# Top-k search of a sparse attention layer: counts, candidates, norm powers and the place of the selections

## The chip, the cores and the metric

The kernel runs on one core of a Trainium2 chip. The metric is the device time of one execution in microseconds (us). TensorE (PE in the profile) multiplies matrices, VectorE (DVE), ScalarE (ACT) and GpSimd (POOL, here "Pool") work element by element, SyncE (SP) issues the transfers. Each engine works through its own queue in order, and waits on semaphores for the others.

## What is computed

Two transformer layers over 1024 tokens of width 1024, in float32. The change lies in the first layer, which has two attentions side by side: A, where an indexer scores every key for each query and only the 256 best keys of the query are attended to, and B, a sliding window. The second layer is not touched.

```python
def layer_ab(x, norm_g, w_in, a_qk_norm, a_kidx_norm, b_qk_norm, b_sinks, w_out):
    y = rms_norm(x, norm_g) @ w_in
    qa, ka, va, qi, ki, wi, za, qb, kb, vb, zb = split_cols(y, AB_SPLITS)
    ...
    qi = apply_rope(qi.reshape(bsz, seq, IDX_HEADS, IDX_DIM), icos, isin)
    ki = apply_rope(rms_norm(ki, a_kidx_norm)[:, :, None, :], icos, isin)[:, :, 0]
    k_sel = min(DSA_TOPK, seq // 4)
    oa = dsa_attention(qa, ka, heads(va, A_KV_HEADS), qi, ki, wi, k_sel)
    ...
    ob = swa_sink_attention(qb, kb, heads(vb, B_KV_HEADS), b_sinks)
    mix = jnp.concatenate([oa * jax.nn.silu(za), ob * jax.nn.silu(zb)], axis=-1)
    return x + mix @ w_out

# in dsa_attention, for each block of 128 queries
        logits = jnp.einsum('bqhd,bsd->bqhs', qib, ki).astype(jnp.float32)
        score = jnp.einsum('bqh,bqhs->bqs', wib, jax.nn.relu(logits)) * idx_scale
        causal = key_pos[None, :] <= t[:, None]
        score = jnp.where(causal[None], score, -jnp.inf)
        _, idx = lax.top_k(score, k_sel)
        ...
        p = masked_softmax(s, valid[:, :, None, None, :])
```

## The kernel before

Tokens are tiled in eight blocks of 128. Projections are done as three products of split operands (`whi`, `wlo` are the two parts of a weight, from L446 on ScalarE and L447 on Pool). The first layer runs in this order: five calls of `norm_x` normalize the input (two per pair of blocks later); the columns `ki` and `qi` are projected; `scores()` computes the index scores of query blocks 2 to 7 (blocks 0 and 1 have no more than 256 keys) and cuts each into two 16-bit halves, `hi` and `lo` (L802 to L819); then the top-k search runs as an auxiliary generator, `tk = topk()`, beside the remaining projections and beside attention B; then attention A.

`Lanes` holds these strands together. `run(main, fill, ratio, aux, arate)` takes steps of a main strand, of a filling strand (projections) and of an auxiliary strand (`tk`) by the costs that each step yields; `post` hands over a short strand, and `tick` advances every posted strand by one step. The order in which the steps are written is the priority; the order on each engine is then fixed by the scheduler of the framework at build time, so it isn't a table that is written by hand.

The search finds, for each query, the 256th largest score by bits: 16 rounds over the `hi` halves, one more count, a masking of the `lo` halves (L877), 16 rounds over `lo`. Each round sets `cand` from the threshold `K` (L850), counts the scores at or above it in six blocks, compares the six counts with their targets (`inc`, L856) and moves `K` (L857). A count of block i reads (i + 1) x 128 columns. `GDA` gives its first list of blocks to VectorE (L845, a comparison with a sum) and its second to ScalarE (L841, a sign with a sum). Before, VectorE counts blocks 2, 3, 4 and 7 (384, 512, 640 and 1024 columns), ScalarE 5 and 6 (768 and 896).

When `K` is found, each block's selection makes its mask: seven VectorE instructions (L889 to L895) and two on Pool (L896, L897), which write the mask over the block's `hi`. Attention A's blocks 2 to 7 wait for their masks, its score reduce is L639 (`nm`) and its scores are L636. In the kernel before, `now(tk)` takes the rest of the search and all six selections to the end before attention A is written.

`rstd` (L270 to L289) turns sums of squares into reciprocal square roots: a start value from the bits of the number and two correction steps, nine small VectorE instructions (L277, L278, L280, L281, L283, L284, L286, L287, L288). In the first layer it is called 33 times: five times by the first norms, 28 times by head chains, the strands that norm and rotate the heads of a projection and end in operands for TensorE (`qs`, `ka`, `kb`; `ss` is their sum of squares, `nz` the normed head). `E` and `ENG` say which of some element-wise steps go to Pool; `ENG2` replaces it for the second layer.

## Time and profile before

| what | us |
|---|---|
| median of three runs (lowest, highest) | 1560.41 (1559.73, 1562.62) |
| the profiled execution | 1559.19 |
| its span | 1557.4 |
| first and last comparison of the search (L856) start at | 179.6 and 413.3 |

The difference between the profiled execution and its span is what lies around the first and last instruction. A row of a table by stretch gives, for one part of the span, the time that each engine was busy; a row of a group of instructions gives its count, busy time and mean, and the idle time of the engine just before them with what ended it. Counts of instructions stand after an x. L numbers are lines of the kernel before.

### The profile page before, as it was taken

The numbers are of one execution on the slowest core, as the hardware profiler recorded it, in microseconds if no ns is written. First come the engines' busy times: TensorE is split into PE (matmuls) and PEld (weight loads), VectorE is DVE, ScalarE is ACT, GpSimd is POOL, SyncE is SP. The second block draws the span as 40 slices with busy tenths as digits, with TensorE's granted clock in tenths as the row PEclk, the third lists the DMA queues.
The fourth block names the chain that finished last, engine by engine and source line by source line (L and its number), as shares of the span: only waits on it lengthen the run. The fifth ranks groups of instructions, "written<-read, shape, count | busy, mean of one in ns | idle before, by whom it ended". The sixth has DMA issues, their size and how long they took to land.

```text
span 1557.4 us, 35155 instructions
## 1 busy us (share of the span) xinstructions
PE 1384.3 (89%) x12588; PEld 1273.9 (82%) x12588; DVE 1226.1 (79%) x3827; ACT 869.8 (56%) x2385; POOL 821.4 (53%) x1097
## 2 busy tenths in 40 slices
PE   6998888788637889999999999999999778889999
PEld 6888878788636779999999998899988556778887
DVE  8599999999998876428338668976689999996763
ACT  6354576577406766325424666956667666754531
POOL 4767642467777657324447343565456565652240
PEclk9999999989867999999999999999999879989999
DMA  6311212111102132332312210012100210111232
GB/s 199 86 35 32 57 56 71 43 36 33 45 17 69 59 107 76 111 108 86 82 36 55 66 49 8 9 47 63 33 15 19 78 62 15 32 55 59 95 112 75
DMA packets 88431, 93.19 MB, mean 60 GB/s; under 512 B 20928, under 2 KB 73152, under 8 KB 88256
## 3 DMA queue, kind: packets, MB, share of 16 engines
q1 hardware_dynamic: 88256, 90.95, 19.3%
q8 instruction: 99, 1.62, 0.4%
q14 instruction: 76, 0.62, 0.1%
HBM read 67.85 MB, written 23.07 MB: 58 GB/s over the span
## 4 chain that ended last, share of the span: by engine, by line
PE 48%; DVE 33%; DMA 6%; POOL 5%; issue 5%; ACT 3%; SPq 0%; POOLq 0%; DVEq 0%; ACTq 0%
PE psS L636 8%; PE pp L490 7%; PE pp L492 6%; PE pp L491 6%; PE psT L664 6%; DVE junk L845 6%; DVE pt L639 4%; PE pp L1683 2%; PE pp L1681 2%; PE pp L1682 2%; PE po L684 2%; PE po L682 2%; PE po L683 2%; DMA wraw<-in_ab_w_in 1%; POOL wlo L447 1%
## 5 line engine op out<-in xcount | busy, mean ns | idle before, releaser
L490 PE MATMUL pp<-whi,Rh 128*128 128x256 f32 (+4 forms) x1648 | 489.1, 297 | 25.9 <-DVE zst L581 9.9
L492 PE MATMUL pp<-whi,Rl 128*128 128x256 f32 (+4 forms) x1648 | 481.0, 292 | 0.6 <-DVE Rl L327 0.6
L491 PE MATMUL pp<-wlo,Rh 128*128 128x256 f32 (+4 forms) x1648 | 480.0, 292 | 0.0
L490 PEld LDWEIGHTS pp<-whi,Rh 128*128 128x128 f32 x1648 | 322.5, 196 | 33.1 <-DVE zst L581 13.9
L644 ACT ACTIVATE pt<-pt,nm 128x256 f32<-128x256 f32 (+8 forms) x384 | 246.6, 643 | 178.6 <-DVE nm L639 173.3
L492 PEld LDWEIGHTS pp<-whi,Rl 128*128 128x128 f32 x1648 | 321.1, 195 | 2.2 <-DVE Rl L327 1.1
L491 PEld LDWEIGHTS pp<-wlo,Rh 128*128 128x128 f32 x1648 | 322.0, 196 | 1.0
L447 POOL TENSOR_TENSOR wlo<-wraw,whi 128x256 fp32r<-128x256 f32 (+4 forms) x208 | 162.3, 787 | 189.6 <-ACT whi L446 176.9
L664 PE MATMUL psT<-identf,pt 128*128 128x128 f32 x1256 | 216.1, 284 | 14.2 <-DVE pl L669 4.2
L674 POOL TENSOR_SCALAR ph<-sg 128x512 f16<-128x512 f32 (+3 forms) x157 | 89.3, 570 | 157.9 <-ACT sg L673 142.0
L664 PEld LDWEIGHTS psT<-identf,pt 128*128 128x128 f32 x1256 | 147.3, 143 | 28.1 <-issue 4.3
L675 POOL TENSOR_TENSOR pl<-sg,ph 128x512 f16<-128x512 f32 (+3 forms) x157 | 163.4, 1041 | 8.7
L446 ACT ACTIVATE whi<-wraw 128x256 fp32r<-128x256 f32 (+4 forms) x208 | 83.7, 416 | 125.0 <-DMA wraw<-in_cd_w_in 37.8
L669 DVE SCALAR_TENSOR_TENSOR pl<-psT,ph 128x512 f16<-128x512 f32 (+3 forms) x233 | 128.4, 556 | 26.8 <-ACT ph L668 26.4
L668 ACT ACTIVATE ph<-psT 128x512 f16<-128x512 f32 (+3 forms) x233 | 111.9, 492 | 51.7 <-PE psT L664 49.2
L684 PEld LDWEIGHTS <-pl 128*128 128x128 f16 x1256 | 114.2, 99 | 26.1 <-issue 7.4
L682 PEld LDWEIGHTS <-ph 128*128 128x128 f16 x1256 | 116.7, 100 | 20.0 <-issue 7.9
L683 PEld LDWEIGHTS <-ph 128*128 128x128 f16 x1256 | 116.7, 100 | 14.7 <-issue 13.5
L639 DVE CUSTOM_DVE_ANT_0 pt<-psS,mk 128x512 f32<-128x512 f32 (+4 forms) x208 | 107.1, 518 | 23.7 <-PE psS L636 21.8
L673 ACT ACTIVATE sg<-psT 128x512 f32<-128x512 f32 (+3 forms) x157 | 83.4, 534 | 32.7 <-PE psT L664 30.1
L344 POOL TENSOR_TENSOR nz<-nz,rs_y 128x512 f32<-128x512 f32 (+2 forms) x44 | 41.2, 937 | 94.0 <-DVE rs_y L288 68.2
L636 PE MATMUL psS<-ka,qs 128*128 128x512 f32 (+4 forms) x192 | 58.7, 405 | 24.1 <-DVE nm L639 23.8
(311 smaller groups left out, 3622.4 us busy)
## 6 DMA issues: line engine op xcount, KB each, us to landing
wraw<-in_cd_w_in SPq DMA_DIRECT2D x72, 128.0 KB, 2.1
wraw<-in_ab_w_in SPq DMA_DIRECT2D x56, 128.0 KB, 2.2
xs<-in_x SPq DMA_DIRECT2D x8, 512.0 KB, 6.0
od<-mx SPq DMA_DIRECT2D x32, 128.0 KB, 1.8
wraw<-in_ab_w_out SPq DMA_DIRECT2D x32, 128.0 KB, 2.2
x<-in_x SPq DMA_DIRECT2D x8, 512.0 KB, 4.6
mo<-od SPq DMA_DIRECT2D x16, 256.0 KB, 2.7
nz<-zdr SPq DMA_DIRECT2D x16, 256.0 KB, 2.8
```

What stands on the lines that cost most here:

```text
L447: G.tensor_tensor(lo[:, :o], raw[:, :o], hi[:, :o].bitcast(F32), OP.subtract)
L490: T.matmul(ps, xh, hi[:, :n], start=q == 0 and k == 0, stop=False)
L491: T.matmul(ps, xh, lo[:, :n], start=False, stop=False)
L492: T.matmul(ps, xl, hi[:, :n], start=False, stop=q == 3 and k == 1)
L636: T.matmul(ps[:, at + a - c:at + b - c], lhs, rhs(a, b), start=n == 0, stop=n == len(pl_) - 1)
L639: V.tensor_tensor_reduce(pt[:, j * nk + c:j * nk + c + w], ps[:, at:at + w], mask(c, w), -1.0, first, op0=OP.add, op1=OP.min, accum_out=low)
L644: S.activation(pt[:, j * nk:(j + 1) * nk], pt[:, j * nk:(j + 1) * nk], AF.Exp, scale=-1.0, bias=nm[:, h:h + 1], accum_out=sm[:, h:h + 1])
L664: T.transpose(pT[:, a], pt[:, o:o + P], identf)
L675: G.tensor_tensor(pl[:, :n], sg[:, :n], ph[:, :n], OP.subtract)
L682: T.matmul(dst, ph[:, a], vh(kt, h), start=kt == 0, stop=False)
L683: T.matmul(dst, ph[:, a], vl(kt, h), start=False, stop=False)
L684: T.matmul(dst, pl[:, a], vh(kt, h), start=False, stop=kt == nt - 1)
```

## The change

There are four parts. (1) `GDA` gives blocks 3 and 4 to ScalarE too, so VectorE counts blocks 2 and 7 and ScalarE blocks 3, 4, 5 and 6. (2) The search carries the candidate itself in place of the threshold: Pool computes `less`, the candidate minus half a step, while the counts run; then `inc` and one VectorE instruction, `cand = inc * step + less`, end the round, in place of `inc`, `K` and `cand`. The comparisons are turned round (less than, and the sign of a negated input), and `K` is made once at the end of each search. (3) In the first layer `rstd` becomes two Pool instructions, a scaling and a power with exponent -0.5 from a constant tile. (4) In place of `now(tk)` the search alone is taken to its end, and the strand with the six selections is posted, so that its steps are written between the steps of attention A.

```diff
--- before.py
+++ after.py
@@ -53,7 +53,7 @@
-GDA = [2, 3, 4, 7], [5, 6]
+GDA = [2, 7], [3, 4, 5, 6]
@@ -70,7 +70,7 @@
-ENG = 'nz zc ky'
+ENG = 'nz zc ky rs'
...
+    half = cst.tile([P, 16], F32, name="half")
+    G.memset(half, -0.5)
@@ -274,6 +276,12 @@
         t = st.tile([P, 16], F32, name="rs_t")[:, :n]
         w = ss.shape[0]
         v, y, t = v[:w], y[:w], t[:w]
+        if E["rs"] is G:
+            G.tensor_scalar(v, ss, inv * RG * RG, EPS * RG * RG, op0=OP.mult, op1=OP.add)
+            G.tensor_tensor(y, v, half[:w, :n], OP.pow)
+            yield
+            res.append(y)
+            return
         V.tensor_scalar(v, ss, inv, EPS, op0=OP.mult, op1=OP.add)
         V.tensor_scalar(y.bitcast(I32), v.bitcast(I32), -0.5, float(0x5F3759DF), op0=OP.mult, op1=OP.add)
         yield
@@ -821,6 +829,8 @@
     GD, GA = GDA
+    searched = []
     def topk():
@@ -833,52 +843,53 @@
         cnt = tkp.tile([P, 6], F32, name="cnt")
         tgt = tkp.tile([P, 6], F32, name="tgt")
         inc = tkp.tile([P, 6], F32, name="inc")
-        sgn = tkp.tile([P, 6], F32, name="sgn")
+        less = tkp.tile([P, 6], F32, name="less")
         def counts(src):
             for i in GA:
                 n = (i + 1) * P
-                S.activation(junka[:, :n], blk(src, i), AF.Sign, bias=cand[:, i - 2:i - 1],
+                S.activation(junka[:, :n], blk(src, i), AF.Sign, scale=-1.0, bias=cand[:, i - 2:i - 1],
                              accum_out=cnt[:, i - 2:i - 1])
             for i in GD:
                 n = (i + 1) * P
-                V.tensor_scalar(junk[:, :n], blk(src, i), cand[:, i - 2:i - 1], None, op0=OP.is_ge, op1=OP.add,
+                V.tensor_scalar(junk[:, :n], blk(src, i), cand[:, i - 2:i - 1], None, op0=OP.is_lt, op1=OP.add,
                                 accum_out=cnt[:, i - 2:i - 1])
-        def setcand(K, b):
-            V.scalar_tensor_tensor(cand, K, float(b), sgn, op0=OP.add, op1=OP.mult)
         def search(K, src):
             for b in range(15, -1, -1):
-                setcand(K, 1 << b)
+                if b:
+                    G.tensor_scalar(less, cand, 1.0, -float(1 << (b - 1)), op0=OP.mult, op1=OP.add)
                 counts(src)
-                V.tensor_tensor(inc, cnt, tgt, OP.is_ge)
-                V.scalar_tensor_tensor(K, inc, float(1 << b), K, op0=OP.mult, op1=OP.add)
+                V.tensor_tensor(inc, cnt, tgt, OP.is_le)
+                if b:
+                    V.scalar_tensor_tensor(cand, inc, float(1 << b), less, op0=OP.mult, op1=OP.add)
+                else:
+                    V.tensor_tensor(cand, inc, cand, OP.add)
                 yield 2000
-        V.memset(K1, -32768.5)
-        V.memset(K0, -0.5)
-        V.memset(tgt, float(TOPK))
-        V.memset(sgn, 1.0)
-        for i in GA:
-            V.memset(tgt[:, i - 2:i - 1], float(2 * TOPK - (i + 1) * P))
-            V.memset(sgn[:, i - 2:i - 1], -1.0)
+            V.tensor_scalar(K, cand, -0.5, None, op0=OP.add)
+        V.memset(cand, -0.5)
+        for i in range(2, NT):
+            n = (i + 1) * P
+            V.memset(tgt[:, i - 2:i - 1], float(n - TOPK if i in GD else n - 2 * TOPK))
         yield from search(K1, hi16)
-        setcand(K1, 1)
         counts(hi16)
         for i in range(2, NT):
             V.tensor_scalar(tgt[:, i - 2:i - 1], cnt[:, i - 2:i - 1], -1.0,
-                            float(TOPK if i in GD else 2 * TOPK - 2 * (i + 1) * P), op0=OP.mult, op1=OP.add)
-        V.tensor_scalar(K1, K1, 0.5, None, op0=OP.add)
+                            2.0 * (i + 1) * P - (TOPK if i in GD else 2 * TOPK), op0=OP.mult, op1=OP.add)
+        V.memset(cand, 32767.5)
         yield 2000
         for i in range(2, NT):
             V.scalar_tensor_tensor(blk(lo16, i), blk(hi16, i), K1[:, i - 2:i - 1], blk(lo16, i),
                                    op0=OP.is_equal, op1=OP.mult)
             yield 800
         yield from search(K0, lo16)
-        V.tensor_scalar(K0, K0, 0.5, None, op0=OP.add)
+        searched.append(1)
         for i in range(2, NT):
             n = (i + 1) * P
@@ -1111,7 +1122,10 @@
     FM = fa_then()
     L.run(attn_gen(jobs(job_b, 0, BO[0]) + jobs(job_b, 1, BO[1])), FA, BR, aux=tk, arate=TA)
-    now(tk)
+    while not searched:
+        next(tk)
+        L.tick()
+    L.post(tk)
     L.run(attn_gen(jobs(job_a, 0, AO[0]) + jobs(job_a, 1, AO[1])), FM, AR)
     L.pump(FM)
     L.flush()
```

The scheduler's order changes with it. VectorE, two rounds late in the search over `lo` before; `rs_v`, `rs_y` and `rs_t` are the norm chain, `ka` a head chain's operand:

```order
L845 TENSOR_SCALAR junk,cnt<-lo_837,cand 128x384
L286 SCALAR_TENSOR_TENSOR rs_t<-rs_y 128x8
L399 TENSOR_TENSOR ka_4544<-psT,ka_4544 128x256
L845 TENSOR_SCALAR junk,cnt<-lo_838,cand 128x512
L287 TENSOR_TENSOR rs_t<-rs_t,rs_v 128x8
L845 TENSOR_SCALAR junk,cnt<-lo_838,cand 128x640
L288 SCALAR_TENSOR_TENSOR rs_y<-rs_t,rs_y 128x8
L338 TENSOR_REDUCE ss<-sq 128x8
L845 TENSOR_SCALAR junk,cnt<-lo_838,cand 128x1024
L277 TENSOR_SCALAR rs_v<-ss 128x8
L856 TENSOR_TENSOR inc<-cnt,tgt 128x6
L278 TENSOR_SCALAR rs_y<-rs_v 128x8
```

VectorE in two late rounds of the changed kernel:

```order
L855 TENSOR_SCALAR junk,cnt<-lo_790,cand 128x384
L855 TENSOR_SCALAR junk,cnt<-lo_791,cand 128x1024
L377 TENSOR_TENSOR qs<-psT,qs 64x512 x2
L346 TENSOR_REDUCE ss<-sq 128x8
L364 TENSOR_TENSOR nz<-nz,rp_t 128x512
L866 TENSOR_TENSOR inc<-cnt,tgt 128x6
L868 SCALAR_TENSOR_TENSOR cand<-inc,less 128x6
L855 TENSOR_SCALAR junk,cnt<-lo_790,cand 128x384
L855 TENSOR_SCALAR junk,cnt<-lo_791,cand 128x1024
L866 TENSOR_TENSOR inc<-cnt,tgt 128x6
L868 SCALAR_TENSOR_TENSOR cand<-inc,less 128x6
L855 TENSOR_SCALAR junk,cnt<-lo_790,cand 128x384
```

The norm chain and two of the four counts are gone, and `nz`, `qs` and `ss` of later head chains stand between the counts.

ScalarE, two rounds late in the search before (`whi` is a weight split, `sg` a copy of scores of attention B, `nz` and `sq` start a head chain):

```order
L841 ACTIVATE junka,cnt<-lo_838,cand 128x768
L422 ACTIVATE nz<-pp 128x256
L424 ACTIVATE sq<-pp 128x256
L841 ACTIVATE junka,cnt<-lo_838,cand 128x896
L673 ACTIVATE sg<-psT 128x512
L841 ACTIVATE junka,cnt<-lo_838,cand 128x768
L422 ACTIVATE nz<-pp 128x256
L424 ACTIVATE sq<-pp 128x256
L446 ACTIVATE whi<-wraw 128x256
L841 ACTIVATE junka,cnt<-lo_838,cand 128x896
L398 ACTIVATE ka_4543<-psT 128x256
L446 ACTIVATE whi<-wraw 128x256
```

ScalarE at the same place in the changed kernel:

```order
L851 ACTIVATE junka,cnt<-lo_791,cand 128x512
L851 ACTIVATE junka,cnt<-lo_791,cand 128x640
L851 ACTIVATE junka,cnt<-lo_791,cand 128x768
L851 ACTIVATE junka,cnt<-lo_791,cand 128x896
L851 ACTIVATE junka,cnt<-lo_791,cand 128x512
L851 ACTIVATE junka,cnt<-lo_791,cand 128x640
L851 ACTIVATE junka,cnt<-lo_791,cand 128x768
L851 ACTIVATE junka,cnt<-lo_791,cand 128x896
L851 ACTIVATE junka,cnt<-lo_791,cand 128x512
L851 ACTIVATE junka,cnt<-lo_791,cand 128x640
L851 ACTIVATE junka,cnt<-lo_791,cand 128x768
L851 ACTIVATE junka,cnt<-lo_791,cand 128x896
```

The counts of several rounds now follow one another with nothing between, and copies that stood between the counts before stand ahead of them.

VectorE in the selection of the second block before:

```order
L889 TENSOR_SCALAR junk<-hi_836,K_1536 128x512
L890 SCALAR_TENSOR_TENSOR sel,cnt<-lo_838,K_1537,junk 128x512
L369 TENSOR_TENSOR qs<-psT,qs 64x512 x2
L891 TENSOR_SCALAR inc<-cnt 128x1
L892 TENSOR_SCALAR junk<-lo_838,K_1537 128x512
L338 TENSOR_REDUCE ss<-sq 128x8
L893 SCALAR_TENSOR_TENSOR sel<-hi_836,K_1536,junk 128x512
L277 TENSOR_SCALAR rs_v<-ss 128x8
L894 SCALAR_TENSOR_TENSOR junk<-sel 128x512
L278 TENSOR_SCALAR rs_y<-rs_v 128x8
L895 SCALAR_TENSOR_TENSOR sel<-junk,inc,sel 128x512
L280 TENSOR_TENSOR rs_t<-rs_y 128x8
```

VectorE in the selections of the changed kernel:

```order
L900 TENSOR_SCALAR junk<-hi_789,K_1454 128x512
L901 SCALAR_TENSOR_TENSOR sel,cnt<-lo_791,K_1455,junk 128x512
L902 TENSOR_SCALAR inc<-cnt 128x1
L903 TENSOR_SCALAR junk<-lo_791,K_1455 128x512
L904 SCALAR_TENSOR_TENSOR sel<-hi_789,K_1454,junk 128x512
L905 SCALAR_TENSOR_TENSOR junk<-sel 128x512
L906 SCALAR_TENSOR_TENSOR sel<-junk,inc,sel 128x512
L900 TENSOR_SCALAR junk<-hi_789,K_1454 128x640
L901 SCALAR_TENSOR_TENSOR sel,cnt<-lo_791,K_1455,junk 128x640
L902 TENSOR_SCALAR inc<-cnt 128x1
L903 TENSOR_SCALAR junk<-lo_791,K_1455 128x640
L904 SCALAR_TENSOR_TENSOR sel<-hi_789,K_1454,junk 128x640
```

The selections follow one another without the norm chains and `qs` that stood between; the score reduces of attention A (`pt,nm`) come in the sixth selection in both orders.

## Rows read from the trace of the kernel before

**Rows 1.** Page of the profile, part 1: busy time, share of the span, instructions.

```profile
PE 1384.3 (89%) x12588; PEld 1273.9 (82%) x12588; DVE 1226.1 (79%) x3827; ACT 869.8 (56%) x2385; POOL 821.4 (53%) x1097
```

**Rows 2.** Table by stretch: stretch, its length, busy times and counts, TensorE clock, DMA.

```profile
0.00:92.00 92.00, 74.69 (x540) 72.02 (x541) 63.76 (x183) 46.11 (x120) 56.07 (x105) 0.96 0.44 132
92.00:180.00 88.00, 74.97 (x535) 70.34 (x534) 85.03 (x180) 38.91 (x108) 59.36 (x70) 0.96 0.13 34
180.00:413.50 233.50, 194.40 (x1653) 185.97 (x1652) 229.11 (x726) 155.80 (x431) 124.26 (x162) 0.93 0.17 49
413.50:475.00 61.50, 25.51 (x162) 23.14 (x160) 61.10 (x101) 10.03 (x29) 47.08 (x42) 0.65 0.11 35
475.00:560.00 85.00, 75.10 (x818) 61.63 (x817) 72.96 (x216) 64.57 (x159) 52.44 (x67) 0.91 0.21 64
```

**Rows 3.** Timeline of VectorE, 0 to 20 us: start, duration, instruction, idle time before.

```profile
5.71 0.15 DVE L277 TENSOR_SCALAR rs_v<-ss 128x1 f32<-128x1 f32 x1 [4.41 <-ACT pt L510]
...
9.89 1.76 DVE L516 SCALAR_TENSOR_TENSOR pt<-xs,rs_y,gx 128x1024 f32<-128x1024 f32 x1
```

**Rows 4.** Busy time by stretch of L277 alone, then of L288 alone.

```profile
92.00:180.00 88.00, 3.10 (x7) 0.96 0.13 34
180.00:413.50 233.50, 4.69 (x12) 0.93 0.17 49
...
92.00:180.00 88.00, 2.01 (x8) 0.96 0.13 34
180.00:413.50 233.50, 1.74 (x11) 0.93 0.17 49
```

**Rows 5.** Groups of VectorE, 180 to 413.5 us: busy, mean, then idle time before.

```profile
L845 DVE TENSOR_SCALAR_CACHE_REDUCE junk<-lo,cand 128x640 bf16<-128x640 uint16 x16 | 13.9, 872 | 0.1
...
L845 DVE TENSOR_SCALAR_CACHE_REDUCE junk<-lo,cand 128x512 bf16<-128x512 uint16 x16 | 11.8, 735 | 0.0
...
L850 DVE SCALAR_TENSOR_TENSOR cand<-K,sgn 128x6 f32<-128x6 f32 x32 | 10.1, 315 | 0.4
```

**Rows 6.** Groups of ScalarE, 180 to 413.5 us.

```profile
L644 ACT ACTIVATE pt<-pt,nm 128x256 f32<-128x256 f32 x53 | 26.8, 506 | 20.5 <-DVE nm L639 20.4
...
L841 ACT ACTIVATE junka<-lo,cand 128x896 int8<-128x896 uint16 x16 | 16.7, 1041 | 0.1
...
L841 ACT ACTIVATE junka<-lo,cand 128x768 int8<-128x768 uint16 x16 | 15.0, 935 | 16.3 <-DVE cand L850 6.9 <-DVE rs_t L280 3.5 <-DVE rs_y L284 1.6
...
L841 ACT ACTIVATION_READ_ACCUMULATOR junka<-lo,cand 128x1 f32 x32 | 6.2, 193 | 0.0
```

**Rows 7.** Groups of VectorE, 413.5 to 475 us.

```profile
L894 DVE TENSOR_TENSOR_SCAN junk<-sel 128x384 f16<-128x384 bf16 (+5 forms) x6 | 10.2, 1706 | 0.0
...
L369 DVE TENSOR_TENSOR qs<-psT,qs 64x512 fp32r<-64x512 f32 x4 | 2.8, 690 | 0.1
L356 DVE TENSOR_TENSOR nz<-nz,rp_t 128x512 f32<-128x512 f32 x4 | 2.7, 676 | 0.0
L281 DVE TENSOR_TENSOR rs_t<-rs_t,rs_v 128x8 f32<-128x8 f32 x3 | 2.0, 683 | 0.0
...
L891 DVE TENSOR_SCALAR inc<-cnt 128x1 f32<-128x1 f32 x6 | 0.9, 146 | 0.0
...
L287 DVE TENSOR_TENSOR rs_t<-rs_t,rs_v 128x8 f32<-128x8 f32 x3 | 0.4, 148 | 0.0
```

**Rows 8.** Waits from 413.5 to 600 us: total, times, longest.

```profile
PE psS L636 <- DVE nm L639: 23.8, 10, 15.9
```

**Rows 9.** Groups of Pool: two sizes of product, the second from 92 to 180 us.

```profile
L320 POOL TENSOR_TENSOR rp_t<-ydup,cs 128x16 f32<-128x16 f32 x8 | 1.9, 235 | 10.4 <-DVE ydup L1379 10.1
...
L322 POOL TENSOR_TENSOR nz<-nz,cs 128x512 f32<-128x512 f32 x4 | 5.7, 1424 | 0.2
```

**Rows 10.** Summary of line L856: duration min/median/max in ns, first and last start.

```profile
L856 DVE TENSOR_TENSOR inc<-cnt,tgt x32: 133/162/1073, 179.6 to 413.3; 128x6 f32<-128x6 f32 x32
```

**Rows 11.** Waits from 180 to 413.5 us: total, times, longest.

```profile
ACT junka L841 <- DVE cand L850: 20.1, 14, 3.6
```

More of the change, by code (lines that the diff above doesn't have):

```diff
@@ L166, in trunk @@
     L = Lanes()
-    E = {n: G if n in ENG.split() else V for n in "nz zc qy ky dk dq dr dy".split()}
+    E = {n: G if n in ENG.split() else V for n in "nz zc qy ky dk dq dr dy rs".split()}
     cst = ctx.enter_context(tc.tile_pool(name="cst", bufs=1))
```

## The prediction

> **What bounds the kernel now.** I read the totals first, then a table of busy times by stretch, then the groups of instructions inside the stretches that the change touches, then the waits. Over the whole span TensorE is the busiest engine [rows 1], and a reader could stop there. The table by stretch says otherwise [rows 2]: from 92 to 180 us (index scores) VectorE is busy 85.0 of 88 us and TensorE 75.0; from 180 to 413.5 us (the search) VectorE 229.1 of 233.5, TensorE 194.4, ScalarE 155.8, Pool 124.3; from 413.5 to 475 us (the selections) VectorE 61.1 of 61.5 and TensorE 25.5 at a clock of 0.65. So these 383 us are VectorE's. Behind 600 us, up to 1200, TensorE is nearly full, and the change touches nothing there; it can only move the start of that part. The question is how much VectorE time leaves these three stretches, and who is next.
>
> The profiled run took 1559.19 us (span 1557.4), the median of the three runs is 1560.41: I make the sum on the profiled run and add 1.2 us at the end.
>
> **First norms, 0 to 92 us.** Nine small VectorE instructions per call become two on Pool. The first chain starts at 5.71 us and the product that uses it at 9.89 [rows 3], 4.2 us with TensorE still waiting for its first operand. Two Pool instructions of about 0.25 us (price below) with their handovers are about 1 us. The first call gains some 3 us; the four that follow overlap with weight loads, and in the Pool order the third and later pairs stand behind weight splits, which takes part of it back. I take **-2** (bounds -5 to +2).
>
> **Index scores, 92 to 180 us.** The nine lines of the norm chain hold VectorE 23.3 us here; first and last of them are in [rows 4] (3.10 and 2.01 us). They go. VectorE then needs 62 of 88 us, TensorE 75.0 and Pool 59.4 plus 16 new instructions, 4 to 8 us. TensorE is next, so at most 88 - 75 = 13 us can go. I take **-10** (bounds -13 to -3: the first score blocks also wait for chains that only got shorter).
>
> **The search, 180 to 413.5 us.** Per round VectorE loses the 512 and the 640 column counts: 0.74 + 0.87 us and one accumulator read each, about 1.65 us, over the 31 rounds here 51 us [rows 5]. It loses one of three small instructions per round, 10.1 us of `cand` lines [rows 5], and the norm chains, 26.6 us (4.69 us in the first of the nine lines, 1.74 in the last [rows 4]). 229 - 51 - 10 - 27 = 141; the order shows some 10 to 20 us of head work (`nz`, `qs`, `ss`) drawn in from the selections, so 150 to 165.
>
> ScalarE gains the two counts. Its counts of 768 and 896 columns take 0.935 and 1.041 us [rows 6], 0.1 us for 128 columns; carried down, 640 and 512 columns take 0.83 and 0.72, each with an accumulator read of 0.19 of which half overlaps: about 1.75 us a round, 54 us. 155.8 + 54 = 210, and the order draws in ten or so copies that stood behind the last count before: about 222 us. **ScalarE is next**, and it is nearly as full as VectorE was. A sum of the rows of each round in the new order gives the same: the larger of the two engines, round by round, adds up to 224 us.
>
> It can't fill every gap. Each round ends with a handover (last count, `inc`, `cand`, first count): an accumulator read of 0.19 us [rows 6], two small instructions of 0.16 [rows 10] and the steps between engines, by my estimate 0.9 us in all. The last rounds have nothing on ScalarE between the counts: 3.9 us of counts and 0.9, about 4.8 us each. Some ten such rounds add 9 us, and the counts stand in order behind exponentials that wait for VectorE (20.5 us of idle time before the group L644 [rows 6]). I take 238 us, **+4**, with bounds 222 (all gaps filled) and 260 (222, and the idle time that the groups of [rows 6] show before them, some 37 us, all stays). So the counts moved to ScalarE hardly pay by themselves: they exchange one full engine for another.
>
> `less` on Pool adds a wait: it needs `cand`, and behind it on Pool stand weight splits, `ph`/`pl` and the norm pairs. It is due only a whole round later and Pool is 53% busy, so I cost it at nothing; if Pool comes late by 1 us in each of 30 rounds, it is 30 us, half of it hidden by ScalarE's own waits.
>
> **The selections, 413.5 to 475 us.** Seven lines, 10.2 us for the longest and 0.9 for the shortest [rows 7], add up to 44.8 us. The other 16 us of VectorE here are norm chains (10.6, nine lines between 2.0 and 0.4), `qs` (2.8), `nz` (2.7) and small things [rows 7]; the norm chains go, the rest now stands ahead of the last counts. The order shows the first five selections in one unbroken block behind `K`, and only the sixth among the first scores of attention A, just as before. So posting them doesn't put them beside attention; the stretch shrinks to its own work: 61.5 to about 44.5, **-17** (bounds -12 to -22, the longer one if the port is quieter).
>
> **Attention A's start, 475 to 560 us.** VectorE 73 of 85 us, TensorE 75 [rows 2]. TensorE's longest wait here is 15.9 us for a score reduce that stands behind the selections [rows 8]; it moves with them and isn't counted again. Two norm chains and `nz` work go: **-4** (0 to -7).
>
> Sum: -2 - 10 + 4 - 17 - 4 = **-29**. 1559.2 - 29 = 1530.2 profiled, **1531** as a median.
>
> **The price of the power.** No row before shows a power on Pool. From below, Pool's smallest products, 128x16, take 0.235 us; from above, its long products, 128x512, 1.42 us [rows 9]. The tile is 128x8 or smaller, so I take 0.25 to 0.5 us, near the lower row; at 1.42 us the shorter chains still beat nine VectorE instructions (3.1 us a call in the scores), and the sum loses about 10 us.
>
> Pool also slows VectorE. `inc` takes 162 ns in the median and up to 1073 [rows 10], and such rows lie beside Pool's instructions. The Trainium skill, "SBUF — State Buffer", section "SBUF: two separate sides", says that the two share a port pair as an exclusive lock: an instruction of one holds back a two-input instruction of the other for its whole length. The trace agrees by the spread of `inc`. By that rule 96 new Pool instructions of 0.25 us could hold VectorE for up to 24 us, most of it where ScalarE is the bound, and the sum would be about -20.
>
> The Trainium skill, "GPSIMD Engine Reference", section "2.1 Instruction dispatch", adds that the first call of freshly loaded code costs about 6 us without an instruction in the profile. No run here shows it; with it the first norm would lose time and the sum would be -23.
>
> **Rivals.**
> A. ScalarE's order rules the search. The in-order counts stand behind work that waits, so the search takes 250 to 262 us, +17 to +28. For it: ScalarE at 95% by my sum, and 20.1 us of waits of the counts for `cand` already [rows 11]. Against: two of its three producers get faster. Sum -16 to -5: 1544 to 1556.
> B. The slow side: the power is long. It stands in 33 head chains, of which about half (5 first norms, 8 in the scores, a few ahead of A) are on the path. The forecast turns at 0.25 + 29/17, about 2 us for one power; at 4 us it is 17 x 3.75 - 29 = +35: 1595. For it: a power is no product, and nothing here prices it. Against: a tile of this size is the smallest that Pool handles, and the row beside it takes 0.235 us [rows 9].
> C. The relief reaches TensorE. If the search falls to its bound of 222 us and the scores to TensorE's 75: -5 - 13 - 11 - 22 - 7 = -58, at most 1502.
> D. The change doesn't do what its last part says, selections beside attention. That is in the forecast already by the order.
>
> **How the numbers follow.** Forecast (-15 to -45 us, 1515 to 1545): 0.55. A: 0.18. B: 0.12, a third of it still under 1557. C: 0.10, 1500 to 1515. Of the rest, 0.05, smaller mishaps that end within 0.2%. The range takes the forecast, A and the better half of C, with the bounds of the power up to 1.4 us: 1506 to 1557, which leaves out about 2 in 10. About 0.2% (3 us) is what a measurement of this kernel can tell from no change. Faster by more: 0.55 + 0.10 + 0.15 of A = 0.80 with rounding; within: 0.07; slower: 0.13.
>
> **What would show it.** Right: first to last `inc` of about 225 to 240 us with VectorE near 70% busy and ScalarE over 90%; the selection block about 45 us with nothing between its lines; 92 to 180 shorter by 10 us with TensorE over 95%; the power's mean under 0.5 us. Wrong: ScalarE idle before its counts for over 1 us a round and a search of 250 us (A); a power of over 2 us and Pool's `nz` late (B); `less` ending after the last count of its round; a TensorE without gaps in the search (C).

## The result: 1543.9 us

The changed kernel takes 1543.87 us in the median of four runs (1541.17 to 1546.13). The kernel before, timed beside it, takes 1561.51 us, so the change is 17.6 us or 1.1% faster: a ratio of 0.9886 (95% interval 0.9865 to 0.9908). The forecast was 1531, in a range from 1506 to 1557. The profiled execution's span is 1542.8 us, 14.6 less than before.

Totals of the page (busy, share of the span, instructions), which answer to [rows 1]:

```profile
PE 1364.3 (88%) x12588; PEld 1261.3 (82%) x12588; DVE 1110.0 (72%) x3365; ACT 919.6 (60%) x2517; POOL 874.4 (57%) x1194
```

VectorE gave up 116 us, ScalarE took 50 and Pool 53. The table by stretch of the changed kernel (columns as in [rows 2]) is cut at the events that end a stage: the first index score on TensorE, the first and last round's `inc`, attention A's first score reduce and its last over a mask.

```profile
0.00:77.90 77.90, 61.18 (x450) 59.16 (x451) 36.74 (x78) 37.15 (x98) 57.98 (x113) 0.98 0.48 146
77.90:174.10 96.20, 86.52 (x638) 81.11 (x637) 77.00 (x123) 50.16 (x134) 84.95 (x99) 1.00 0.16 41
174.10:417.30 243.20, 201.47 (x1786) 193.88 (x1784) 176.67 (x484) 210.81 (x579) 183.58 (x257) 0.91 0.18 51
417.30:452.30 35.00, 0.00 (x0) 0.00 (x0) 33.67 (x45) 0.00 (x0) 14.57 (x12) 0.50 0.00 0
452.30:605.10 152.80, 136.81 (x1497) 120.08 (x1498) 113.25 (x331) 105.23 (x255) 98.31 (x122) 0.93 0.27 79
605.10:1542.80 937.70, 878.29 (x8223) 807.08 (x8221) 672.69 (x2307) 516.21 (x1454) 435.04 (x595) 0.97 0.19 57
```

In the search (third row) VectorE is busy 177 of 243 us in place of 229 of 233.5, ScalarE 211, TensorE 201. In the selections (fourth row) VectorE is full and has only Pool's masks beside it: TensorE and ScalarE have 0.00 us, and TensorE's clock is 0.50 of full speed, the lower of its two levels (1.2 of 2.4 GHz). The same cuts in both kernels, beside the forecast's terms, whose stages ended at nearby times (92, 180, 413.5, 475 and 560 us of the kernel before):

| stage | before | after | change | forecast |
|---|---|---|---|---|
| start to first index score (80.2, 78.1 us) | 80.2 | 78.1 | -2.1 | -2 |
| to the first `inc` (179.6, 174.1) | 99.4 | 96.0 | -3.4 | -10 |
| first to last `inc` (413.3, 417.0) | 233.7 | 242.9 | +9.2 | +4 |
| to attention A's first reduce (467.2, 452.3) | 53.9 | 35.3 | -18.6 | -17 |
| to the end of the span (1557.4, 1542.8) | 1090.2 | 1090.5 | +0.3 | -4 |
| sum | 1557.4 | 1542.8 | -14.6 | -29 |

Most search rounds now end when ScalarE's last count does. The summary of the changed line of `inc` (duration min/median/max in ns, first and last start, then what its engine waited for in us and times):

```profile
L866 DVE TENSOR_TENSOR inc<-cnt,tgt x32: 164/304/1126, 174.1 to 417.0; 128x6 f32<-128x6 f32 x32
...
  ACT junka L851: 43.2, 27
```

The waits of the search (us in total, times, longest):

```profile
DVE inc L866 <- ACT junka L851: 43.2, 27, 3.5
...
POOL less L863 <- DVE cand L868: 16.9, 9, 7.9
ACT junka L851 <- DVE cand L868: 13.1, 16, 1.8
ACT pt L652 <- DVE nm L647: 12.9, 11, 4.2
```

VectorE stands 43.2 us for ScalarE's last count, in 27 of the 32 rounds; the counts in turn wait 13.1 us for `cand`, in place of 20.1 [rows 11], and Pool 16.9 us at `less`. The two new counts and the exponentials among them (groups of ScalarE in the search: busy, mean in ns, idle time before):

```profile
L652 ACT ACTIVATE pt<-pt,nm 128x256 f32<-128x256 f32 x54 | 27.4, 510 | 12.0 <-DVE nm L647 11.8
...
L851 ACT ACTIVATE junka<-lo,cand 128x640 int8<-128x640 uint16 x16 | 13.2, 825 | 0.3
...
L851 ACT ACTIVATE junka<-lo,cand 128x512 int8<-128x512 uint16 x16 | 11.6, 727 | 10.6 <-DVE cand L868 10.6
```

0.825 and 0.727 us are what the slope of [rows 6] had given (0.83 and 0.72). What was far off is the power. Groups of Pool for its line by size:

```profile
L281 POOL TENSOR_TENSOR rs_y<-rs_v,half 128x8 f32<-128x8 f32 x16 | 26.9, 1680 | 0.3
...
L281 POOL TENSOR_TENSOR rs_y<-rs_v,half 128x4 f32<-128x4 f32 x8 | 8.9, 1107 | 0.2
...
L281 POOL TENSOR_TENSOR rs_y<-rs_v,half 128x2 f32<-128x2 f32 x7 | 4.9, 702 | 0.3
...
L281 POOL TENSOR_TENSOR rs_y<-rs_v,half 128x1 f32<-128x1 f32 x2 | 1.1, 566 | 0.2
```

The first two powers in Pool's timeline, the first with its scaling (start, duration, idle time before):

```profile
5.83 0.19 POOL L280 TENSOR_SCALAR rs_v<-ss 128x1 f32<-128x1 f32 x1 [4.67 <-ACT pt L518]
6.10 0.57 POOL L281 TENSOR_TENSOR rs_y<-rs_v,half 128x1 f32<-128x1 f32 x1
...
9.73 0.56 POOL L281 TENSOR_TENSOR rs_y<-rs_v,half 128x1 f32<-128x1 f32 x1
```

The power takes 0.57 us for one column and 1.68 for eight, 33 times, 42 us of Pool; the forecast had taken 0.25 to 0.5 us, with 1.42 as the upper end.

### The profile page after: what moved, and what is told of

It reads as the page before. It is cut to its first block, busy times and chain, and to the rows that moved or that the text cites. A ratio compares the mean times of both kernels' runs of the same rounds, so it can differ in the third digit from the quotient of the medians.

```text
span 1542.8 us, 34986 instructions
## 1 busy us (share of the span) xinstructions
PE 1364.3 (88%) x12588; PEld 1261.3 (82%) x12588; DVE 1110.0 (72%) x3365; ACT 919.6 (60%) x2517; POOL 874.4 (57%) x1194
## 4 chain that ended last, share of the span: by engine, by line
PE 53%; DVE 24%; ACT 8%; DMA 5%; issue 5%; POOL 4%; SPq 1%; POOLq 0%; DVEq 0%; ACTq 0%
PE pp L498 8%; PE pp L500 8%; PE pp L499 8%; PE psS L644 8%; PE psT L672 6%; ACT junka L851 4%; DVE pt L647 4%; PE pp L1697 2%; PE pp L1695 2%; PE pp L1696 2%; PE po L692 2%; PE po L690 2%; DVE pl L677 2%; PE po L691 2%; DMA wraw<-in_ab_w_in 1%
## 5 line engine op out<-in xcount | busy, mean ns | idle before, releaser
L498 PE MATMUL pp<-whi,Rh 128*128 128x256 f32 (+4 forms) x1648 | 483.4, 294 | 17.3 <-ACT sq L432 7.9
L498 PEld LDWEIGHTS pp<-whi,Rh 128*128 128x128 f32 x1648 | 317.1, 193 | 23.7 <-ACT sq L432 9.5
L499 PEld LDWEIGHTS pp<-wlo,Rh 128*128 128x128 f32 x1648 | 316.8, 192 | 3.5 <-POOL wlo L455 2.3
L500 PEld LDWEIGHTS pp<-whi,Rl 128*128 128x128 f32 x1648 | 316.3, 192 | 1.2
L455 POOL TENSOR_TENSOR wlo<-wraw,whi 128x256 fp32r<-128x256 f32 (+4 forms) x208 | 164.6, 799 | 138.2 <-ACT whi L454 131.3
L683 POOL TENSOR_TENSOR pl<-sg,ph 128x512 f16<-128x512 f32 (+3 forms) x157 | 163.8, 1044 | 9.0
L644 PEld LDWEIGHTS psS<-ka,qs 128*128 128x128 f32 x192 | 32.9, 211 | 56.1 <-DVE nm L647 55.0
```

The costliest lines, as they stand in the source:

```text
L455: G.tensor_tensor(lo[:, :o], raw[:, :o], hi[:, :o].bitcast(F32), OP.subtract)
L498: T.matmul(ps, xh, hi[:, :n], start=q == 0 and k == 0, stop=False)
L499: T.matmul(ps, xh, lo[:, :n], start=False, stop=False)
L500: T.matmul(ps, xl, hi[:, :n], start=False, stop=q == 3 and k == 1)
L644: T.matmul(ps[:, at + a - c:at + b - c], lhs, rhs(a, b), start=n == 0, stop=n == len(pl_) - 1)
L683: G.tensor_tensor(pl[:, :n], sg[:, :n], ph[:, :n], OP.subtract)
```

## Experiments

Each run is set against the kernel before, timed beside it on the same chip. A time is a median; a ratio to the kernel before has its 95% interval. Not all runs lie on one chip (e11 to e13 lie on another than the other experiments), so two runs are compared by their ratios where it matters; 0.001 is 1.6 us. Line numbers are those of the changed kernel. Each edit also lets the scheduler set a new order, so a run shows an edit together with its order.

**The order with and without part 4.** The change's last part posts the selections beside attention A. With `now(tk)` put back into the changed kernel, the instructions of all five engines stand in the same order, row for row. By the code, `pump` ticks every posted strand while it waits for a projection, so the selections are all written early. The part does nothing, and the kernel without it was not run.

**The counts as before (e1).**

```diff
-GDA = [2, 7], [3, 4, 5, 6]
+GDA = [2, 3, 4, 7], [5, 6]
```

> The changed kernel with the old split of the counts (VectorE counts blocks 2, 3, 4 and 7, ScalarE 5 and 6); all else stays changed. Theory: the search of the changed kernel (first to last L866: 242.9 us) is ScalarE's (210.8 of 243.2 us busy, VectorE 176.7), and moving the counts back makes it VectorE's again: 176.7 + 51 = 228 us of VectorE, so the search takes 232 to 240 us and the whole kernel 1540 to 1550; part 1 is worth nothing by itself. Rival: the room on VectorE is what let TensorE do its work ahead of the selections, so with the old split head work comes back between the selections, their stretch grows from 35 to 45 us or more and the kernel takes 1552 to 1560.

1544.43 us, 0.9897 (0.9876 to 0.9918): the same as the whole change. So part 1 is worth nothing by itself, as the theory had it. But the stages look unlike what the theory had expected; the rival had the mechanism (head work comes back between the selections) but not the time. Search and selections by stretch:

```profile
174.90:374.30 199.40, 164.41 (x1415) 156.13 (x1414) 192.68 (x577) 144.78 (x398) 119.46 (x176) 0.93 0.18 51
374.30:450.40 76.10, 36.21 (x303) 33.47 (x302) 56.22 (x76) 16.41 (x46) 73.36 (x67) 0.71 0.14 45
```

The search falls to 199 us, and the 36 us of TensorE's work that the changed kernel does in it comes back into the selections, 76 us long, where Pool is busy 73.4 of 76.1. The sum of both stretches is 275.5 us, against 278.2 in the changed kernel. The two stretches are one pool of work; a split moves the border and the engine that is full.

**The norms on VectorE (e2).**

```diff
-ENG = 'nz zc ky rs'
+ENG = 'nz zc ky'
```

> The changed kernel with the first layer's norms back on VectorE as nine small instructions; all else stays changed. Theory: the norms are the part that pays; without it the score stretch is 5 us longer, VectorE has 27 us more in the search (204 of 243, still under ScalarE's 211) and 10 us more in the selections: 1552 to 1560. Rival: the power on Pool (median 1554 ns, 33 times, 43 us of Pool in all) sits in the head chains and costs as much as it gives; then without it the kernel takes 1535 to 1545.

1555.69 us, 0.9967 (0.9952 to 0.9982): the norms on Pool are worth 12 us, and the rival falls. Its stretches:

```profile
181.60:436.40 254.80, 199.23 (x1801) 191.78 (x1799) 208.04 (x610) 212.84 (x579) 163.75 (x230) 0.91 0.17 49
436.40:470.10 33.70, 0.00 (x0) 0.00 (x0) 32.37 (x44) 0.00 (x0) 13.87 (x10) 0.50 0.00 0
```

The selections take 33.7 us here too, with the norm chains still on VectorE. So the norms' leaving isn't what shortened them. The split is, since e1, which takes only the split back, has 76 us: while ScalarE's slower search runs, VectorE and TensorE do the head work that stood between the selections before.

**Three blocks on VectorE (e4).**

```diff
-GDA = [2, 7], [3, 4, 5, 6]
+GDA = [2, 3, 7], [4, 5, 6]
```

> The changed kernel with only block 4 moved to ScalarE: VectorE counts blocks 2, 3 and 7, ScalarE 4, 5 and 6. VectorE then has 177 + 25 = 202 us in the search and ScalarE 211 - 30 = 181. Theory (ScalarE is next, and the change moved one block too many): the search falls from 243 to 222 to 232 us and the kernel to 1525 to 1534. Rival (the search is paced by the handovers between the engines and by TensorE's 201 us, whichever engine counts): the search stays at 238 to 245 and the kernel at 1540 to 1546.

1536.39 us, 0.9843 (0.9824 to 0.9861), about 7 us faster than the whole change and a little above the theory's range. Search and selections:

```profile
175.80:391.30 215.50, 186.76 (x1696) 181.15 (x1696) 187.18 (x536) 182.66 (x501) 156.31 (x225) 0.93 0.20 57
391.30:436.80 45.50, 17.73 (x108) 16.68 (x108) 43.05 (x55) 4.79 (x12) 40.90 (x34) 0.65 0.02 6
```

The search falls by 28 us, more than the 11 to 21 expected, with VectorE and ScalarE equally busy (187 and 183), and 10 us go back to the selections. Both stretches take 261.0 us in place of 278.2. The rival (handovers set the pace) falls. ScalarE was next in the changed kernel, and the change moved one block too many.

**A cheap power (e6).** A product stands in place of Pool's power, so the first layer's norms are left out.

```diff
-            G.tensor_tensor(y, v, half[:w, :n], OP.pow)
+            G.tensor_tensor(y, v, half[:w, :n], OP.mult)
```

> The changed kernel with a product in place of Pool's power, so the norms of the first layer are left out (the instruction stays, with another operation). It shows what the power's length costs. Theory: the power's 0.6 to 1.7 us against about 0.25 us for a product takes some 40 us of Pool's time, of which a third is on the path, mostly in the score stretch (Pool 71 of 82 us): 1526 to 1536. Rival: the power is hidden, since Pool isn't the bound: 1541 to 1546.

1538.42 us, 0.9856 (0.9839 to 0.9873), between the two ranges. The line's groups by size:

```profile
L281 POOL TENSOR_TENSOR rs_y<-rs_v,half 128x8 f32<-128x8 f32 x16 | 3.4, 214 | 0.4
...
L281 POOL TENSOR_TENSOR rs_y<-rs_v,half 128x4 f32<-128x4 f32 x8 | 2.6, 327 | 0.3
```

The summary of `inc`, with its first and last start:

```profile
L866 DVE TENSOR_TENSOR inc<-cnt,tgt x32: 154/167/1191, 169.1 to 414.2; 128x6 f32<-128x6 f32 x32
```

The power's length costs about 5 us. The intervals just overlap, but the trace bears it out: the first round starts at 169.1 us, and in the nine kernels with the power between 173.8 and 176.8 (174.1 in the changed kernel). So nearly all of it lies ahead of the search. The two stages there:

```profile
0.00:74.70 74.70, 60.24 (x447) 57.81 (x448) 36.87 (x78) 36.61 (x94) 53.40 (x112) 0.98 0.51 152
74.70:169.10 94.40, 84.07 (x624) 78.28 (x623) 77.56 (x122) 50.15 (x137) 75.42 (x101) 1.00 0.16 40
```

The first index score comes 3.4 us earlier than in the changed kernel, and the score stretch is 1.6 us shorter. Against the kernel before, the two stages would have come out at -5.5 and -5.0 us: in sum close to the forecast of -12, but not one by one (-2 and -10). The search itself is no shorter (245.1 us).

**The candidate alone (e5)**: the kernel before with part 2 only. As an edit of the changed kernel:

```diff
-GDA = [2, 7], [3, 4, 5, 6]
+GDA = [2, 3, 4, 7], [5, 6]
-ENG = 'nz zc ky rs'
+ENG = 'nz zc ky'
...
-    while not searched:
-        next(tk)
-        L.tick()
-    L.post(tk)
+    now(tk)
```

> The kernel before with the candidate carried in place of the threshold and nothing else (old split of the counts, norms on VectorE, selections in the old place). VectorE loses one small instruction per round, 10 us, in a stretch where it is full (282.9 of 287.6 us from the first round to attention A's first score reduce). Theory: 6 to 10 us of it come through, 1549 to 1555. Rival: Pool's added instruction and the handover at each round's end eat it, 1557 to 1562.

1551.61 us, 0.9950 (0.9933 to 0.9967): 8 us, as the theory had it. VectorE is still full in both stretches, search and selections, 273.0 of 278.9 us:

```profile
179.70:392.70 213.00, 177.62 (x1515) 167.86 (x1513) 207.54 (x668) 151.21 (x415) 118.92 (x179) 0.94 0.18 51
392.70:458.60 65.90, 34.13 (x267) 32.67 (x266) 65.46 (x109) 13.38 (x36) 49.61 (x44) 0.74 0.12 39
```

**The norms alone (e10)**: part 3 put into the kernel before. Its main lines:

```diff
-ENG = 'nz zc ky'
+ENG = 'nz zc ky rs'
...
+        if E["rs"] is G:
+            G.tensor_scalar(v, ss, inv * RG * RG, EPS * RG * RG, op0=OP.mult, op1=OP.add)
+            G.tensor_tensor(y, v, half[:w, :n], OP.pow)
+            yield
+            res.append(y)
+            return
```

> The kernel before with the first layer's norms as two Pool instructions and nothing else. VectorE loses 37 us between the first round and attention A's first score reduce, and some 20 us in the score stretch. Theory: VectorE was the only bound there, so 20 us or more come through and the kernel takes 1532 to 1541, less than the whole change, since the counts moved to ScalarE give nothing. Rival: the power's 1.1 to 1.7 us in the head chains and TensorE at 95% of the score stretch leave 8 to 14 us: 1546 to 1552, and the change needs its other parts.

1541.89 us, 0.9873 (0.9838 to 0.9908). One part of four gives all that the change gives (the intervals overlap). The time lies between the two ranges, a microsecond from the theory's. Search and selections:

```profile
176.00:388.60 212.60, 174.63 (x1504) 164.91 (x1504) 207.18 (x616) 148.81 (x411) 122.83 (x160) 0.94 0.18 50
388.60:444.70 56.10, 26.70 (x212) 25.14 (x211) 51.05 (x68) 11.84 (x32) 52.69 (x45) 0.70 0.15 49
```

VectorE is busy 258.2 of 268.7 us: 25 us left it, and 19 came through.

**The selections truly beside attention A (e8).** 16 empty steps follow each selection.

```diff
-    L.post(tk)
+    def spaced(gen, k):
+        for _ in gen:
+            for _ in range(k):
+                yield
+
+    L.post(spaced(tk, 16))
```

> The changed kernel with 16 empty steps behind each selection, so that its order has three selections ahead of attention A's first score reduce, and three among A's first blocks (the changed kernel has all but the last ahead; its order is that of the kernel with the selections in the old place). Theory: during the selections TensorE and ScalarE have nothing at all (0 us busy in 35), so work of A beside them is gained: A's first reduce comes some 18 us earlier, the later selections take about 15 us of VectorE beside A, where VectorE is 75 to 85% busy: 1529 to 1537. Rival: VectorE needs the same time for A's reduces and the selections in any order, and is the bound there: 1540 to 1546.

1539.67 us, 0.9866 (0.9837 to 0.9895), between the two ranges, with an interval that overlaps that of the whole change. Search, selections ahead of A's first reduce, and from there to A's last reduce:

```profile
175.40:418.60 243.20, 200.14 (x1785) 192.78 (x1784) 176.40 (x484) 211.12 (x579) 183.76 (x257) 0.91 0.18 51
418.60:437.40 18.80, 0.00 (x0) 0.00 (x0) 18.03 (x29) 0.00 (x0) 7.51 (x8) 0.50 0.00 0
437.40:602.70 165.30, 139.94 (x1497) 123.34 (x1498) 126.86 (x346) 106.94 (x255) 110.81 (x126) 0.89 0.24 73
```

A's first reduce comes 15 us earlier (the theory had 18), but the stretch behind it is 165.3 us in place of 152.8, since VectorE now does 14 us of selections there. Most is given back; what is left, 3 to 4 us, isn't clear of the measurement.

**Three blocks and spaced selections (e9)**: the edits of e4 and e8 together.

> Only block 4 moved to ScalarE, and the selections spaced as in the run before. Theory: the two gains add, 7.5 us from the split and what spacing gives: 1520 to 1530. Rival: with the balanced split head work lies between the selections again (TensorE 17.7 of 45.5 us busy there), so spacing gives less: 1530 to 1537.

1527.99 us, 0.9790 (0.9761 to 0.9818): 32 us faster than before, about 15 faster than the whole change, and 8 faster than e4 alone. The theory's range holds it. The same three stretches:

```profile
176.80:392.30 215.50, 186.68 (x1697) 180.96 (x1696) 187.41 (x536) 182.71 (x501) 156.45 (x225) 0.93 0.20 57
392.30:418.30 26.00, 17.70 (x108) 16.66 (x108) 23.95 (x37) 4.79 (x12) 21.80 (x21) 0.76 0.03 10
418.30:589.40 171.10, 141.14 (x1498) 121.77 (x1499) 133.53 (x350) 107.98 (x255) 129.89 (x145) 0.89 0.23 71
```

**The smaller candidate on VectorE (e11, e12).** `less` on VectorE, in e1 and in e9.

```diff
-                    G.tensor_scalar(less, cand, 1.0, -float(1 << (b - 1)), op0=OP.mult, op1=OP.add)
+                    V.tensor_scalar(less, cand, 1.0, -float(1 << (b - 1)), op0=OP.mult, op1=OP.add)
```

> The kernel of the run with the counts of before (candidate carried, norms on Pool, old split), with the one instruction that makes the smaller candidate on VectorE in place of Pool. Theory: on Pool it waits for the candidate at the head of an in-order queue (31.9 us of idle time, 21 waits), so weight splits and head work pile up behind it and Pool is busy 73 of the 76 us of the selections; with it on VectorE the stretch from the first round to attention A's first score reduce falls from 275.5 to 262 to 268 us and the kernel from 1544.4 to 1533 to 1540. Rival: Pool's wait is idle time of an engine that isn't the bound, and VectorE gets 6 to 10 us more to do: 1544 to 1552.

> The kernel with three blocks on VectorE and the selections spaced by 16 steps (1528.0 us), with the smaller candidate made on VectorE. VectorE is busy 187 of 215.5 us in its search and gets about 6 us more; Pool loses 23 us of waits for the candidate. Theory: 1519 to 1525. Rival: Pool has room here (178 of 241.5 us), and nothing changes: 1526 to 1530.

e11 takes 1550.84 us, 0.9949 (0.9932 to 0.9967), by ratio 8 us more than e1: the rival. My theory of Pool's wait falls: without it Pool is as full in the selections, and TensorE waits for it. The search takes 209.9 us in place of e1's 199.2. The stretch of the selections in e11:

```profile
384.00:457.00 73.00, 33.95 (x266) 31.88 (x265) 56.12 (x70) 13.49 (x37) 71.61 (x64) 0.67 0.15 48
```

TensorE's longest wait in it:

```profile
PE po L692 <- POOL pl L683: 22.5, 3, 11.1
```

e12 takes 1525.10 us, 0.9792 (0.9762 to 0.9821), by ratio the same as e9: the rival. Where VectorE isn't full in the search (187 of 215.5 us), the place of `less` doesn't matter; where it is (193 of 199.4 us in e1), one more instruction per round costs some 8 us.

**Wider spacing (e13)**: 48 steps in place of 16 in e9.

> The kernel with three blocks on VectorE and the selections spaced by 48 steps in place of 16, so that one selection is ahead of attention A's first score reduce instead of three. Theory: TensorE has 8 us without work in the 26 us ahead of that reduce and VectorE is 78% busy behind it, so a few us more come: 1522 to 1527. Rival: the large blocks' masks come later than A needs them, and A waits: 1529 to 1536.

1538.26 us, 0.9881 (0.9848 to 0.9913), by ratio 14 us more than e9: the rival, by more than its range. ScalarE's exponentials wait for A's reduces, which stand behind late selections; the first row is e13's, the second e9's, over the stretch from the last round to A's last reduce.

```profile
ACT pt L652 <- DVE nm L647: 60.7, 29, 9.5
```

```profile
ACT pt L652 <- DVE nm L647: 32.0, 21, 10.7
```

## Why the forecast was right in sign and too large

The stretch from the first round to attention A's first reduce, in eight of the kernels (us of length and of busy time):

| kernel | length | TensorE | VectorE | ScalarE | Pool |
|---|---|---|---|---|---|
| before | 287.6 | 216.6 | 282.9 | 163.9 | 163.8 |
| candidate alone (e5) | 278.9 | 211.8 | 273.0 | 164.6 | 168.5 |
| norms alone (e10) | 268.7 | 201.3 | 258.2 | 160.7 | 175.5 |
| norms and candidate (e1) | 275.5 | 200.6 | 248.9 | 161.2 | 192.8 |
| candidate and split (e2) | 288.5 | 199.2 | 240.4 | 212.8 | 177.6 |
| whole change | 278.2 | 201.5 | 210.3 | 210.8 | 198.1 |
| three blocks (e4) | 261.0 | 204.5 | 230.2 | 187.5 | 197.2 |
| three blocks, spaced (e9) | 241.5 | 204.4 | 211.4 | 187.5 | 178.3 |

- **What bounds the kernel** was right: VectorE was full, and taking work from it pays while it stays full (e5: 10 of it, 9 of time; e10: 25 and 19). From e1 on it isn't full any more, and 73 us less on VectorE than before (whole change) buy 9.
- **First norms, -2**: -2.1 measured. The product that uses the first norm starts at 7.73 us in place of 9.89 [rows 3]. The agreement is luck in part: the power took more than its price here too, and with a product in its place (e6) the stage would have been -5.5.
- **Index scores, -10**: -3.4 measured, and two steps failed. One is the price of the power, taken as 0.25 to 0.5 us from the lower row of [rows 9]; it takes 1.1 us for four columns and 1.7 for eight, the latter above even the upper row. e6 shows what that costs: 5 us ahead of the search, of which only 1.6 lie in this stage. The other step is larger: the sum let TensorE, named as next, fill most gaps of the stage. It doesn't in the changed kernel (86.5 of 96.2 us, with Pool busy 88%), nor in e6, where neither TensorE (84 of 94.4 us) nor VectorE (78) nor Pool (75) is full and the stage is still 5 us longer than forecast. What holds it there wasn't tried.
- **The search, +4**: +9.2, between the value taken and the bound of +26. ScalarE is next, as forecast, at 211 us where the sum had 222. The step that was mis-sized is its idle time: 32 us, where the sum had 16 (222 of 238). 13.1 of them are counts that wait for `cand` and 12.9 exponentials that wait for attention B's score reduce, with the counts in order behind them. That is rival A's mechanism in part: the search ended at 243 us, not at its 250 to 262, and its sign (over 1 us idle before the counts of a round) didn't come, with 0.4.
- **The selections, -17**: -18.6, right in size by luck and wrong in its reason. I had the norm chains leave; e2 keeps them on VectorE and has the same 34 us, and e1 moves them and has 76. Search and selections share their work, so my two terms weren't independent: what left the selections made the search longer. Another 6 us come from the selections' own seven lines, which I had left at 44.8 us: from the first to the last of them they are busy 44.9 us before and 39.1 in the changed kernel, while Pool is busy 46.8 of 61.3 us and 17.1 of 43.8. A quieter Pool as the reason would fit, but wasn't tried. The first of the seven shows it most (duration min/median/max in ns; the kernel before, then the changed one):

```profile
L889 DVE TENSOR_SCALAR junk<-hi,K x6: 315/1284/2199, 413.4 to 462.6; 128x384 bf16<-128x384 int16 x1, 128x512 bf16<-128x512 int16 x1, 128x640 bf16<-128x640 int16 x1, 128x768 bf16<-128x768 int16 x1
```

```profile
L900 DVE TENSOR_SCALAR junk<-hi,K x6: 386/442/1100, 415.4 to 449.0; 128x384 bf16<-128x384 int16 x1, 128x512 bf16<-128x512 int16 x1, 128x640 bf16<-128x640 int16 x1, 128x768 bf16<-128x768 int16 x1
```

- **Attention A's start, -4**: +0.3. From A's first reduce to its last the changed kernel takes 152.8 us in place of 158.5, so 5.7 us came. They are gone within the next 200 us, where TensorE is nearly full in both (the kernel before, then the changed one):

```profile
625.70:820.00 194.30, 193.20 (x1614) 190.16 (x1612) 92.51 (x278) 72.70 (x195) 72.28 (x106) 0.98 0.28 86
```

```profile
605.10:805.00 199.90, 195.78 (x1629) 192.74 (x1628) 92.02 (x276) 72.93 (x196) 73.29 (x107) 0.97 0.28 84
```

TensorE idles 4.1 us there in place of 1.1 and is busy 2.6 us longer, at a granted clock that is a little lower. The cause wasn't tried. From A's last reduce to the end, a part that no edit touches, the thirteen profiles take 931.7 to 938.2 us; these two take 931.7 and 937.7, so the loss need not be the change's.

- **`less` at nothing**: held (e12, and e11, where moving it away cost time), and its alternative price (Pool coming late) was not seen; nobody waited for `less`.
- **Selections beside attention**: the order showed that it doesn't happen, and A starts behind five selections. TensorE waits 46.5 us in one piece for A's first reduce, from before the search's end:

```profile
PE psS L644 <- DVE nm L647: 51.1, 8, 46.5
```

With spacing and the balanced split it does happen, and pays 8 us (e9).
- **Rival B** (a long power) had the right kind of surprise and too high a price: at 1.68 us the power costs about 5 us (e6), not 17 x 1.4 = 24. That most of the 33 chains have slack is the likely reason.

By the lock rule of the Trainium skill ("SBUF — State Buffer", section "SBUF: two separate sides") the sum would have been about -20. The median of `inc` did rise, from 162 to 304 ns [rows 10], but all 32 take 14.0 us in place of 10.5, so at most 3.5 us of the +9.2 lie there. The number of new Pool instructions isn't the reason: e6 has as many, with a median of 167. The timeline of the changed kernel shows what is (start, duration):

```profile
203.21 1.17 POOL L683 TENSOR_TENSOR pl<-sg,ph 128x512 f16<-128x512 f32 x1
...
203.27 1.13 DVE L866 TENSOR_TENSOR inc<-cnt,tgt 128x6 f32<-128x6 f32 x1
```

```profile
402.07 1.63 POOL L281 TENSOR_TENSOR rs_y<-rs_v,half 128x8 f32<-128x8 f32 x1
...
402.21 0.17 DVE L866 TENSOR_TENSOR inc<-cnt,tgt 128x6 f32<-128x6 f32 x1 [0.99 <-ACT junka L851]
```

Each of the 21 `inc` that started while a Pool instruction of another kind (`pl`, `ph`, `wlo`, `nz`, `cs`) had 0.1 us or more to go ended 0.01 to 0.03 us behind it, as the rule says. The one `inc` and the two `cand` that started within a power took 0.16 to 0.17 us, as with Pool idle, and so did six such instructions in e10: the power didn't hold VectorE back, against the rule. So the price that the rule had put on the new instructions did not come.

The rule of the first call ("GPSIMD Engine Reference", section "2.1 Instruction dispatch") doesn't show: the first power takes 0.57 us, as the second does, and starts 0.27 us after its scaling. A load that ended before the scaling would be hidden in the 4.67 us in which Pool waits for ScalarE.

Of the signs that were named, an unbroken selection block and VectorE's share of the search came (73% for 70). ScalarE's share (87% for over 90%), TensorE's in the scores (90% for over 95%) and the power's mean (1.27 us for under 0.5) did not.

Open: why norms with the candidate (e1, 0.9897) aren't faster than norms alone (e10, 0.9873), though VectorE has 9 us less to do. The intervals overlap; Pool is fuller in e1's selections, and e11 showed that the wait of `less` isn't the reason.

## What to carry to other kernels

When work leaves a full engine, price what the next engine gets by a table over the whole region that shares the work, not stage by stage: the balanced split (e4, 187 and 183 us) beat the one that emptied VectorE (177 and 211). A strand that is "posted beside" another is beside it only if the order says so; here a spacing of 16 steps and one block moved back made 1528 us from 1544. An operation that no row prices should be measured, or its upper bound taken beyond the longest row.

## What the hardware showed

A power on Pool costs 0.57, 0.70, 1.11 and 1.68 us for 1, 2, 4 and 8 columns of 128 rows, about 0.16 us per column on 0.4; a product in its place takes 0.21 us for eight columns (e6). `inc`, 128x6 with two inputs, took 0.16 to 0.17 us with Pool idle or in a power, and up to 1.13 us when it started within one of Pool's longer instructions of other kinds, behind whose end it ended by 0.01 to 0.03 us. TensorE's clock was at 0.50 in the 35 us in which it had no matmul (0.67 in the stretch of the selections before, where it was busy 21.8 of 53.7 us), and 0.93 on the mean of the stretch behind. The stretch before:

```profile
413.50:467.20 53.70, 21.77 (x149) 20.41 (x147) 53.35 (x85) 8.05 (x21) 39.52 (x38) 0.67 0.06 20
```
